# Seven products instead of eight for the keys and for half of the depth of queries and gates

## The chip, the core and the metric

The kernel runs on one core of one Trainium2 chip. The metric is the time of one execution on the device in microseconds (us), taken as the median of several runs. A core has a matrix engine (TensorE, PE in the profile; its weight loads are a row of their own, PEld), a vector engine (VectorE, DVE), a scalar engine (ScalarE, ACT), GpSimd (POOL, hardly used here) and SyncE (SP), whose queue issues all the DMA transfers of this kernel. Each engine takes its instructions strictly in the order in which they were put. Matmuls read SBUF and add into banks of PSUM (128 partitions x 512 fp32 values each); DVE and ACT read the banks.

## What is computed

A sequence of 512 tokens of width 2048 goes through an mLSTM layer, then a band-attention layer with 16 heads of 128. All is fp32. The part around the change:

```python
hkv = modulate(rmsnorm(x, kv_g), kmod[:, :D_MODEL], kmod[:, D_MODEL:])
kv = hkv @ kv_w
k_sh = kv[..., :B_WIDTH].reshape(Bn, S, B_HEADS, B_DH)
v_sh = kv[..., B_WIDTH:].reshape(Bn, S, B_HEADS, B_DH)
...
qz = h @ w_in
q = qz[..., :B_WIDTH].reshape(B, S, B_HEADS, B_DH)
z = qz[..., B_WIDTH:]
o = chunk_band_attention(q, k, v, rel_table)
y = o.reshape(B, S, B_WIDTH) * jax.nn.silu(z)
return y @ w_out
```

`kv_w` and `w_in` of this layer are 2048 x 4096 each, `w_out` is 2048 x 2048.

## The kernel before

**Products.** Every fp32 operand of a large product is split in two: `split` (L152) has ACT cast it to fp32r (the high part, `hi`) and DVE subtract that from it (the low part, `lo`). `mm3` (L176) then makes three matmuls, hi x hi, hi x lo and lo x hi. A matmul takes 128 x 128 weights and streams up to 512 columns past them.

**Weights.** All weights lie in DRAM in the order of use (`stream`, L42). `wpiece` (L158) loads the next piece, 128 x 1024 fp32 (512 KB), into one of three `raw` buffers, and splits it into one of three `hi` and `lo` buffers. It is put ahead of other work by a priority (`AHEAD`), so a scheduler, which fixes the order on each engine when the program is built, lets it run up to three pieces ahead of PE.

**Projections.** `proj_a` (L192) makes a transposed tile: 128 output columns x 512 tokens in one PSUM bank, over 16 blocks of depth with 128 each, two pieces of eight blocks. `proj_b` (L195) makes four (or two) tiles of 128 tokens x 512 output columns at once, two blocks of depth to a piece. `psP` has five banks for such tiles, `psA` three for all else.

**Stages** (the time of each in the profiled execution stands in the table below): start and the mLSTM heads; its output projection (`rows`); *values* of groups 0 and 1, in two pairs of token tiles (`values`, L680), among which the second half of the tokens is turned and made into `hkv` (`turned`, L621); *keys*, 16 tiles by `proj_a` (L694); values of groups 2 and 3; meanwhile `h2`, the input of queries and gates, is made tile by tile (L701), in the slots that `hkv` leaves free; *attention*, a loop over heads (L792); the output projection and the end. Keys and values of all heads stay in SBUF (`kv`).

In a turn `h` of the loop stand `queries(h)` (one tile by `proj_a`), `mixed(h - 2)` (weights times values, gate, the split of `y2`), `weights(h - 1)` (scores `ps_s`, softmax), `gated(h)` (another tile by `proj_a`, silu) and `flipped(h - 1)` (transposes `ps_t`, splits of the weights and the values).

## Time and profile before

| | us |
|---|---|
| median of 3 runs (2862.17 to 2864.84) | 2862.86 |
| the profiled execution | 2862.53 |
| its span, first to last instruction | 2860.7 |
| output projection of the mLSTM | 1543 to 1896 |
| values, groups 0 and 1 | 1896 to 1989 |
| keys | 1989 to 2163 |
| values, groups 2 and 3 | 2163 to 2250 |
| attention | 2250 to 2688 |
| output projection and end | 2688 to 2861 |

In rows of the profile, a name such as `ps_k<-hkv,wh` says what is written and what is read, without buffer numbers; `128x512 f32` is partitions x elements. The mean time of an instruction is from its start to its end; matmuls are pipelined, so one starts before the one ahead of it has ended. Idle time in front of an instruction is put down to what released it.

### The profile page before, as it was taken

Reading aid. Unit: us, or ns where it says so; the run is one execution under the profiler, and the core shown is the slowest. Engines: PE = TensorE matmul, PEld = TensorE weight load, DVE = VectorE, ACT = ScalarE, POOL = GpSimd, SP = SyncE. Lnnn points to the kernel's source line nnn. Section 1 sums busy time; section 2 is a strip of 40 time slices with the busy share of each in tenths; the row PEclk is TensorE's granted clock in tenths of the full one; section 3 lists DMA queues with packets and bytes.
Section 4 is the critical chain, followed back from the end, with each engine's and each line's share of the span. In section 5 each row is a group of like instructions: output and inputs, shape, how many; then the busy total and the mean of one; then the engine's idle time right before and its main releaser. Section 6 shows DMA issues by size and latency. Waiting matters only on the chain.

```text
span 2860.7 us, 33028 instructions
## 1 busy us (share of the span) xinstructions
PE 2832.2 (99%) x12770; PEld 2340.4 (82%) x12770; DVE 1587.4 (55%) x2358; ACT 1126.1 (39%) x1646; POOL 0.2 (0%) x4
## 2 busy tenths in 40 slices
PE   7999999999999999999999999999999999999998
PEld 5787888888888888888888888888888888888887
DVE  7986747466375564764735445575222455545425
ACT  4244524333242342332424345454222445545323
POOL 0000000000000000000000000000000000000000
PEclk9999999999999999999999999999999999999999
DMA  8874546456456464554635557786222322222334
GB/s 307 310 235 159 192 158 211 168 173 209 155 184 213 136 225 155 195 203 154 209 108 177 180 195 238 231 274 217 96 99 103 138 92 86 90 91 88 137 103 173
DMA packets 154950, 491.09 MB, mean 172 GB/s; under 512 B 17012, under 2 KB 26132, under 8 KB 154280
## 3 DMA queue, kind: packets, MB, share of 16 engines
q1 hardware_dynamic: 154792, 488.98, 50.2%
q8 instruction: 100, 1.64, 0.2%
q14 instruction: 58, 0.48, 0.0%
HBM read 467.89 MB, written 26.26 MB: 173 GB/s over the span
## 4 chain that ended last, share of the span: by engine, by line
PE 93%; DVE 3%; DMA 2%; issue 1%; ACT 1%; SPq 0%; DVEq 0%; ACTq 0%
PE ps_y L174 17%; PE ps_z L174 17%; PE ps_o L174 12%; PE ps_v L174 12%; PE ps_qk L174 9%; PE ps_q L174 6%; PE ps_k L174 6%; PE ps_kv L174 5%; PE ps_l L174 2%; PE ps_s L174 2%; PE ps_n L174 2%; PE ps_lead L174 1%; DVE wl L154 1%; DVE ada L245 1%; DMA wr<-in_wst 1%
## 5 line engine op out<-in xcount | busy, mean ns | idle before, releaser
L154 DVE TENSOR_TENSOR wl<-wr,wh 128x1024 fp32r<-128x1024 f32 (+3 forms) x586 | 680.4, 1162 | 1078.1 <-ACT wh L153 1077.6
L153 ACT CAST wh<-wr 128x1024 fp32r<-128x1024 f32 (+3 forms) x586 | 587.3, 1003 | 1433.0 <-PE ps_y L174 235.6
L174 PE MATMUL ps_y<-wh,y 128*128 128x512 f32 x1536 | 475.2, 390 | 0.0
L174 PE MATMUL ps_z<-h,wh 128*128 128x512 f32 x1408 | 433.9, 389 | 0.0
L174 PEld LDWEIGHTS ps_y<-wh,y 128*128 128x128 f32 x1536 | 288.2, 188 | 59.2
L174 PE MATMUL ps_v<-wh,h 128*128 128x512 f32 x1024 | 317.2, 389 | 0.0
L174 PEld LDWEIGHTS ps_z<-h,wh 128*128 128x128 f32 x1408 | 263.3, 188 | 54.0
L174 PE MATMUL ps_y<-wl,y 128*128 128x512 f32 x768 | 299.1, 389 | 0.0
L174 PE MATMUL ps_o<-h,wh 128*128 128x512 f32 x896 | 276.2, 389 | 0.0
L174 PE MATMUL ps_z<-h,wl 128*128 128x512 f32 x704 | 274.1, 389 | 0.0
L174 PE MATMUL ps_qk<-h,wh 128*128 128x512 f32 x768 | 237.8, 391 | 0.0
L174 PEld LDWEIGHTS ps_v<-wh,h 128*128 128x128 f32 x1024 | 192.1, 188 | 39.8
L174 PE MATMUL ps_v<-wl,h 128*128 128x512 f32 x512 | 199.4, 390 | 0.0
L174 PEld LDWEIGHTS ps_o<-h,wh 128*128 128x128 f32 x896 | 167.3, 188 | 34.1
L245 DVE CUSTOM_DVE_ANT_0 ada<-ada,scB,mod 128x1024 f32<-128x1024 f32 x128 | 164.1, 1282 | 24.2 <-DMA ada<-in_adaT 22.7
L174 PE MATMUL ps_o<-h,wl 128*128 128x512 f32 x448 | 174.4, 389 | 0.0
L174 PEld LDWEIGHTS ps_y<-wl,y 128*128 128x128 f32 x768 | 144.2, 188 | 30.0
L245 DVE CUSTOM_DVE_ANT_0 ada<-ada,scB,cl 128x1024 f32<-128x1024 f32 x128 | 164.0, 1282 | 6.0 <-DMA ada<-in_adaT 5.9
L174 PEld LDWEIGHTS ps_qk<-h,wh 128*128 128x128 f32 x768 | 143.2, 188 | 29.1
L174 PE MATMUL ps_q<-h,wh 128*128 128x512 f32 x512 | 159.3, 392 | 0.0
L174 PE MATMUL ps_kv<-wh,hkv 128*128 128x512 f32 x512 | 159.2, 391 | 0.0
L174 PE MATMUL ps_k<-hkv,wh 128*128 128x512 f32 x512 | 157.5, 389 | 0.0
(216 smaller groups left out, 3389.0 us busy)
## 6 DMA issues: line engine op xcount, KB each, us to landing
wr<-in_wst SPq DMA_DIRECT2D x520, 512.0 KB, 3.3
ada<-in_adaT SPq DMA_DIRECT2D x256, 512.0 KB, 5.4
yr<-ysc SPq DMA_DIRECT2D x16, 512.0 KB, 3.6
wr<-in_wst SPq DMA_DIRECT2D x30, 256.0 KB, 4.5
ysc<-so SPq DMA_DIRECT2D x28, 256.0 KB, 5.3
wr<-in_wst SPq DMA_DIRECT2D x16, 384.0 KB, 5.4
bsc<-in_ext SPq DMA_DIRECT2D x16, 320.0 KB, 6.1
xt<-in_xT SPq DMA_DIRECT2D x4, 1024.0 KB, 7.0
```

Of the source, the lines that this page charges most:

```text
L153: nc.scalar.copy(hi, src)
L154: nc.vector.tensor_tensor(lo, src, hi.bitcast(F32), op=ALU.subtract)
L174: nc.tensor.matmul(ps, a, b, start=start, stop=stop)
L245: pin(nc.vector.tensor_tensor_reduce(at, at, scB[:, j * D // 2 : (j + 1) * D // 2], 1.0, mod[:, i : i + 1] if j else col(CB + i), ALU.mult ...
```

## The change

Take two blocks of depth and two tiles of output columns as a 2 x 2 matrix of weight blocks, and the two blocks of depth and two halves of the tokens as a 2 x 2 matrix of inputs. Their product takes eight block products; in Winograd's form of Strassen's method it takes seven, of sums and differences of the blocks. A block product is a matmul of 128 x 128 weights and 256 tokens, here three of them (`mm3`).

`KEY_PAIRS` says for each of the eight pairs of key tiles how many of the eight pairs of depth blocks are done with seven products: 4, 6, and then all 8. `ATT_PAIRS` says the same for the pair of query and gate tile of a head: 4 of 8. The rest goes as before, with matmuls of 512 columns, into two of the same banks.

- `proj_s` makes a pair of tiles in four banks D, C, A and B, and puts the result together in an SBUF tile `z` (one copy and five sums).
- `half_sums`, called by `key_sums` and `query_sums`, makes the four sums of input halves for a pair of depth blocks and splits them. Four pairs for the keys are made among the values, the other four among the first two pairs of keys; four for the attention among values 2 and 3.
- `wpiece(mat, ns, ...)` makes the three weight sums of `ns` pairs in a piece with three subtractions and additions on DVE, and splits them.
- Room in SBUF: keys, values and `y2` go to DRAM and are loaded again per head (`fetch`) or per two heads (`y2_tile`); `ones_r`, `maskd`, `x2` and the pools `wp`, `rp`, `t2` move.
- The loop over heads: `queries(h, mid)` makes query and gate as one pair; `mixed(h - 2)` and `weights(h - 1)` are called in it ahead of its third piece, `flipped(h - 1)` behind it. `gated` is gone.

The diff, cut to its core:

```diff
+KEY_PAIRS = [4, 6, 8, 8, 8, 8, 8, 8]
+ATT_PAIRS = 4
...
+def pair_pieces(f):
+    sk, nk = list(range(f)), list(range(f, KT // 2))
+    n = min(len(sk), len(nk))
+    out = [([a], [b]) for a, b in zip(sk, nk)]
+    out[1:1] = [([], nk[i : i + 2]) for i in range(n, len(nk), 2)]
+    return out + [(sk[i : i + 2], []) for i in range(n, len(sk), 2)]
...
+            if ns:
+                w = ns * P
+                t = pl.tile([P, 3 * w], F32, tag="ws", name=f"ws{i}", bufs=2)
+                nc.vector.tensor_tensor(t[:, : 2 * w], raw[:, w : 3 * w], raw[:, : 2 * w], op=ALU.subtract)
+                nc.vector.tensor_tensor(raw[:, w : 2 * w], t[:, w : 2 * w], raw[:, :w], op=ALU.add)
+                nc.vector.tensor_tensor(t[:, 2 * w :], raw[:, 3 * w : 4 * w], raw[:, w : 2 * w], op=ALU.subtract)
             hi = wp.tile([P, 1024], F32R, tag="hi", name=f"wh{i}")[:, :n]
             lo = wp.tile([P, 1024], F32R, tag="lo", name=f"wl{i}")[:, :n]
             split(hi, lo, raw)
+            if ns:
+                sh = pl.tile([P, 3 * w], F32R, tag="wsh", name=f"wsh{i}", bufs=bufs)
+                sl = pl.tile([P, 3 * w], F32R, tag="wsl", name=f"wsl{i}", bufs=bufs)
+                split(sh, sl, t)
+                return hi, lo, sh, sl
...
+    def proj_s(mat, xs, ss, f, z, name, pl, bufs, at={}):
+        D, C, A, B = [newp(f"ps_{n}{name}") for n in "dcab"]
...
+            def seven():
+                end = i == len(pieces) - 1
+                for ps, cols, b0, x, xcols, last in (
+                    (D, h1_, ns, lambda k: ss[k][1], h0, False),
+                    (D, h0, 0, lambda k: xs[2 * k], h0, end),
+                    (C, h0, -2 * ns, lambda k: ss[k][0], h1_, False),
+                    (C, h1_, -3 * ns, lambda k: ss[k][0], h0, end),
+                    (A, h0, 3 * ns, lambda k: xs[2 * k + 1], h0, False),
+                    (A, h1_, -ns, lambda k: xs[2 * k + 1], h1_, end),
+                    (B, h0, 2 * ns, lambda k: ss[k][1], h1_, end),
+                ):
...
+                    for j, k in enumerate(sk):
+                        acc(ps, cols, b0 + j, x(k), xcols, last and j == ns - 1)
...
+        with tc.high_priority(AHEAD):
+            nc.scalar.copy(z[:, 0, :], D[:, h0])
+            nc.vector.tensor_tensor(z[:, 3, :], z[:, 0, :], D[:, h1_], op=ALU.add)
+            nc.vector.tensor_tensor(
+                z[:, 1:3, :], z[:, 3:4, :].to_broadcast([P, 2, 256]), C.rearrange("p (a t) -> p a t", a=2), op=ALU.add
+            )
+            nc.vector.tensor_tensor(z[:, 3, :], z[:, 1, :], C[:, h1_], op=ALU.add)
+            nc.vector.tensor_tensor(z[:, 0:2, :], z[:, 0:2, :], A.rearrange("p (a t) -> p a t", a=2), op=ALU.add)
...
+    def half_sums(raw, tmp, pl, tag, name, bufs=KT):
+        (a11, a21), (a12, a22) = ((r[:, :256], r[:, 256:]) for r in raw)
+        (s1, s3), (s2, s4) = ((t[:, :256], t[:, 256:]) for t in tmp)
+        nc.vector.tensor_tensor(s1, a21, a22, op=ALU.add)
+        nc.vector.tensor_tensor(s3, a11, a21, op=ALU.subtract)
+        nc.vector.tensor_tensor(s2, a22, s3, op=ALU.subtract)
+        nc.vector.tensor_tensor(s4, a12, s2, op=ALU.subtract)
...
+            s = pl.tile([P, 2, S], F32R, tag=tag, name=f"{name}_{i}", bufs=bufs)
+            split(s[:, 0, :], s[:, 1, :], t)
...
-        for p, m in zip(pv, ms):
-            for j in range(4):
-                nc.scalar.copy(kv[4 * g + j][:, 1, m * P : (m + 1) * P], p[:, j * P : (j + 1) * P])
...
+            nc.scalar.copy(v, p)
+            nc.sync.dma_start(vsc[g][:, :, m * P : (m + 1) * P], v.rearrange("p (j t) -> p j t", j=4))
...
-    for i in range(KT):
-        ps = newp(f"ps_k{i}")
-        proj_a("kv_w", hkv, ps)
-        nc.scalar.copy(kv[i][:, 0, :], ps)
...
+    for i in range(KT // 2):
+        z = zp.tile([P, 4, 256], F32, tag="z", name=f"zk{i}")
+        ready = len(hs)
+        at = {j: lambda: key_sums(len(hs)) for j in (1, 2)} if ready < KT // 2 else {}
+        assert ready == KEY_PAIRS[i]
+        proj_s("kv_w", hkv, hs, ready, z, f"k{i}", zp, 2, at)
+        nc.sync.dma_start(ksc[i].rearrange("p a t -> p (a t)"), z.rearrange("p a t -> p (a t)"))
...
-    def queries(h):
-        ps = newp(f"ps_q{h}")
-        proj_a("b_w_in", h2, ps)
...
+    def queries(h, mid):
+        if h < BH - 1:
+            fetch(h + 1)
+        z = at.tile([P, 4, 256], F32, tag="z", name=f"z{h}", bufs=2)
+        proj_s("b_w_in", h2, h2s, ATT_PAIRS, z, f"z{h}", at, 3, {2: mid})
...
-        t = kp.tile([P, 2, S], F32R, tag="k", name=f"y2_{h}")
-        split(t[:, 0, :], t[:, 1, :], sz)
-        y2.append(t)
+        nc.sync.dma_start(y2c[h // 2][:, h % 2, :], sz)
...
+    def y2_tile(k):
+        while len(y2) <= k:
+            i = len(y2) // 2
+            raw = wp.tile([P, 2, S], F32, tag="raw", name=f"y2r{i}")
+            nc.sync.dma_start(raw, y2c[i])
+            for j in range(2):
+                t = xp.tile([P, 2, S], F32R, tag="x", name=f"y2_{i}_{j}")
+                split(t[:, 0, :], t[:, 1, :], raw[:, j, :])
+                y2.append(t)
+        return y2[k]
```

More of the change, by code (lines that the diff above doesn't have):

```diff
@@ L39, with add, tile_s @@
 LATER += [DK, DK + P, V0 // 2 + DK, V0 // 2 + DK + P]
+KEY_PAIRS = [4, 6, 8, 8, 8, 8, 8, 8]
[6 more added lines that the diff above has]
+    return out + [(sk[i : i + 2], []) for i in range(n, len(sk), 2)]
 def stream():
     out = []
+    def add(mat, kts, cs):
+        out.append((mat, [(k, c, n) for k in kts for c, n in cs]))
     def tile_a(mat, col, kts=KT):
         for k in range(0, kts, 8):
-            out.append((mat, list(range(k, k + 8)), [(col, P)]))
+            add(mat, range(k, k + 8), [(col, P)])
     def tile_b(mat, col, kts=KT):
         for k in range(0, kts, 2):
-            out.append((mat, [k, k + 1], [(col, 512)]))
+            add(mat, [k, k + 1], [(col, 512)])
+    def tile_s(mat, c1, c2, f):
+        for sk, nk in pair_pieces(f):
+            blocks = [(2 * k + i, c, P) for i, c in ((0, c1), (0, c2), (1, c2), (1, c1)) for k in sk]
+            out.append((mat, blocks + [(2 * k + i, c, P) for k in nk for i in range(2) for c in (c1, c2)]))
     for k0, k1 in BLOCKS:
         for k in range(k0, k1):
-            out.append(("a_w_in", [k], [(c, P) for c in LEAD]))
+            add("a_w_in", [k], [(c, P) for c in LEAD])
         for c in LATER:
-            out.append(("a_w_in", list(range(k0, k1)), [(c, P)]))
+            add("a_w_in", range(k0, k1), [(c, P)])
     for h in range(NH):
@@ L74, in stream @@
             tile_b("kv_w", D + g * 512)
-    for i in range(KT):
-        tile_a("kv_w", i * P)
+    for i in range(KT // 2):
+        tile_s("kv_w", 2 * i * P, (2 * i + 1) * P, KEY_PAIRS[i])
     for g in range(2, 4):
@@ L79, in stream @@
     for h in range(BH):
-        tile_a("b_w_in", h * P)
-        tile_a("b_w_in", D + h * P)
+        tile_s("b_w_in", h * P, D + h * P, ATT_PAIRS)
     for g in range(3):
@@ L86, in stream @@
     return out
-def sizes():
-    return [len(kts) * sum(n for _, n in cs) for _, kts, cs in stream()]
 CB = 0
@@ L111, in hybrid_trunk @@
     dram = ctx.enter_context(tc.tile_pool(name="scr", bufs=1, space=bass.MemoryType.DRAM))
-    wp = ctx.enter_context(tc.tile_pool(name="wp", bufs=3))
     xp = ctx.enter_context(tc.tile_pool(name="xp", bufs=KT))
@@ L115, in hybrid_trunk, with pool @@
     psA = ctx.enter_context(tc.tile_pool(name="psA", bufs=3, space=bass.MemoryType.PSUM))
-    def pool(name, bufs=1):
-        return tc.tile_pool(name=name, bufs=bufs, reuse_waits="tile")
+    def pool(name, bufs=1, **kw):
+        return tc.tile_pool(name=name, bufs=bufs, reuse_waits="tile", **kw)
+    wp = ctx.enter_context(tc.tile_pool(name="wp", bufs=3, side="right"))
     ysc = dram.tile([NH, P, 4, S], F32, name="ysc")
@@ L125, in hybrid_trunk @@
     bsc = dram.tile([BH, P, EXTW], F32, name="bsc")
+    ksc = [dram.tile([P, 2, S], F32, name=f"ksc{i}") for i in range(BH // 2)]
+    vsc = [dram.tile([P, 4, S], F32, name=f"vsc{g}") for g in range(4)]
+    y2c = [dram.tile([P, 2, S], F32, name=f"y2c{i}") for i in range(BH // 2)]
     cl = const.tile([P, NCOL], F32, name="cl")
-    kcs = const.tile([P, 272], F32, name="kcs")
+    kcs = const.tile([P, 144], F32, name="kcs")
     ones_f = const.tile([P, P], F32, name="ones_f")
-    ones_r = const.tile([P, P], F32R, name="ones_r")
     cst = const.tile([P, 4], F32, name="cst")
@@ L138, in hybrid_trunk @@
     nc.vector.memset(ones_f, 1.0)
-    nc.vector.memset(ones_r.bitcast(F32), 1.0)
     nc.vector.memset(cst[:, 0:1], EPS)
@@ L143, in hybrid_trunk @@
     ident = kcs[:, 0:128]
-    maskd = kcs[:, 128:256]
-    sel = kcs[:32, 256:272]
+    sel = kcs[:32, 128:144]
     def col(i):
@@ L156, in hybrid_trunk, with wpiece @@
     ahead = [0]
-    def wpiece(mat):
+    def wpiece(mat, ns=0, pl=None, bufs=2):
         i, at = wpos
-        m, kts, cs = order[i]
+        m, blocks = order[i]
         assert m == mat
-        n = len(kts) * sum(w for _, w in cs)
+        n = sum(w for _, _, w in blocks)
         wpos[:] = i + 1, at + P * n
@@ L167, in wpiece @@
             nc.sync.dma_start(raw, wst[at : at + P * n].rearrange("(p n) -> p n", p=P))
+            out = []
+            if ns:
[4 more added lines that the diff above has]
+                nc.vector.tensor_tensor(t[:, 2 * w :], raw[:, 3 * w : 4 * w], raw[:, w : 2 * w], op=ALU.subtract)
             hi = wp.tile([P, 1024], F32R, tag="hi", name=f"wh{i}")[:, :n]
@@ L214, in proj_b, with acc, eight @@
             held.clear()
+    def proj_s(mat, xs, ss, f, z, name, pl, bufs, at={}):
+        D, C, A, B = [newp(f"ps_{n}{name}") for n in "dcab"]
+        pieces = pair_pieces(f)
+        begun = set()
+        h0, h1_ = slice(0, 256), slice(256, 512)
+        for i, (sk, nk) in enumerate(pieces):
+            if i in at:
+                at[i]()
+            ns = len(sk)
+            parts = wpiece(mat, ns, pl, bufs)
+            def acc(ps, cols, b, x, xcols, last):
+                start = id(ps) not in begun
+                begun.add(id(ps))
+                hi, lo = parts[:2] if b >= 0 else parts[2:]
+                w0 = (b if b >= 0 else b + 3 * ns) * P
+                w = slice(w0, w0 + P)
+                mm3(ps[:, cols], hi[:, w], lo[:, w], x[:, 0, xcols], x[:, 1, xcols], start, last)
+            def eight():
+                for m, k in enumerate(nk):
+                    for j in range(2):
+                        for t, ps in enumerate((A, B)):
+                            acc(ps, slice(0, S), 4 * ns + 4 * m + 2 * j + t, xs[2 * k + j], slice(0, S), False)
+            def seven():
[9 more added lines that the diff above has]
+                ):
+                    if i == 0 and ps is B:
+                        eight()
+                    for j, k in enumerate(sk):
+                        acc(ps, cols, b0 + j, x(k), xcols, last and j == ns - 1)
+            if i:
+                eight()
+            seven()
+        with tc.high_priority(AHEAD):
[6 more added lines that the diff above has]
+            nc.vector.tensor_tensor(z[:, 0:2, :], z[:, 0:2, :], A.rearrange("p (a t) -> p a t", a=2), op=ALU.add)
+            if f < KT // 2:
+                nc.vector.tensor_tensor(z[:, 2:4, :], z[:, 2:4, :], B.rearrange("p (a t) -> p a t", a=2), op=ALU.add)
+            else:
+                nc.vector.tensor_tensor(z[:, 2, :], z[:, 2, :], B[:, h0], op=ALU.add)
@@ new lines, in half_sums @@
+    def half_sums(raw, tmp, pl, tag, name, bufs=KT):
[5 more added lines that the diff above has]
+        nc.vector.tensor_tensor(s4, a12, s2, op=ALU.subtract)
+        out = []
+        for i, t in enumerate(tmp):
+            s = pl.tile([P, 2, S], F32R, tag=tag, name=f"{name}_{i}", bufs=bufs)
+            split(s[:, 0, :], s[:, 1, :], t)
+            out.append(s)
+        return out
@@ L270, in hybrid_trunk @@
             pin(nc.sync.dma_start(cl, cols))
-    pin(nc.sync.dma_start(kcs, kc))
+    pin(nc.sync.dma_start(kcs, kc[:, :144]))
     early = [ada_load(KT, j, ap_, ADA_BUFS, pin) for j in range(2)]
@@ L337, in hybrid_trunk @@
     aT = hp.tile([P, 4, NH], F32, name="aT")
+    ones_r = hp.tile([P, P], F32R, name="ones_r")
+    nc.vector.memset(ones_r.bitcast(F32), 1.0)
+    maskd = hp.tile([P, P], F32, name="maskd")
+    nc.sync.dma_start(maskd, kc[:, 144:272])
     graw = tp.tile([P, KT, 16], F32, tag="t", name="graw")
@@ L560, in hybrid_trunk @@
     kp = kst.enter_context(pool("kp", bufs=KT))
+    tst = ExitStack()
+    tp = tst.enter_context(pool("t2", bufs=6, side="right"))
     rst = ExitStack()
-    rp = rst.enter_context(pool("rp", bufs=12))
-    tst = ExitStack()
-    tp = tst.enter_context(pool("t2", bufs=6))
+    rp = rst.enter_context(pool("rp", bufs=12, side="right"))
     ys = []
@@ L675, in hybrid_trunk @@
             rows(g, ms, ys, at)
-    kv = [kp.tile([P, 2, S], F32, tag="k", name=f"kv{h}") for h in range(BH)]
     def values(g, ms, at={}):
@@ L682, in values, with key_sums @@
         proj_b("kv_w", hkv, pv, ms=ms, at=at)
-        for p, m in zip(pv, ms):
-            for j in range(4):
-                nc.scalar.copy(kv[4 * g + j][:, 1, m * P : (m + 1) * P], p[:, j * P : (j + 1) * P])
+        for i, (p, m) in enumerate(zip(pv, ms)):
+            if g < 2:
+                v = tp.tile([P, S], F32, tag="t", name=f"v{g}_{m}")
+            else:
+                if i % 2 == 0:
+                    z = zp.tile([P, 2, S], F32, tag="z", name=f"v{g}_{m}")
+                v = z[:, i % 2, :]
+            nc.scalar.copy(v, p)
+            nc.sync.dma_start(vsc[g][:, :, m * P : (m + 1) * P], v.rearrange("p (j t) -> p j t", j=4))
+    hs = []
+    def key_sums(k):
+        raw = [kept(2 * k + i, slice(0, S)) for i in range(2)]
+        for i, r in enumerate(raw):
+            c = KT + 2 * k + i
+            nc.scalar.activation(r, r, AF.Identity, bias=mod[:, 80 + c : 81 + c], scale=amul[:, c : c + 1])
+        tmp = [tp.tile([P, S], F32, tag="t", name=f"hs{k}_{i}") for i in range(2)]
+        hs.append(half_sums(raw, tmp, kp, "k", f"hs{k}"))
     with tc.high_priority(AHEAD):
@@ L692, in hybrid_trunk, with query_sums @@
             turn = {4 * i: lambda i=i: turned(1, [i], True) for i in range(4)} if pair == 0 and g == 1 else {}
+            if pair:
+                turn = {k: lambda k=k: key_sums(2 * g + k // 8) for k in (4, 12)}
             values(g, ms, turn)
-    for i in range(KT):
-        ps = newp(f"ps_k{i}")
-        proj_a("kv_w", hkv, ps)
-        nc.scalar.copy(kv[i][:, 0, :], ps)
+    rst.close()
+    zst = ExitStack()
+    zp = zst.enter_context(pool("zp", bufs=2, side="right"))
+    for i in range(KT // 2):
+        z = zp.tile([P, 4, 256], F32, tag="z", name=f"zk{i}")
[4 more added lines that the diff above has]
+        nc.sync.dma_start(ksc[i].rearrange("p a t -> p (a t)"), z.rearrange("p a t -> p (a t)"))
+    kst.close()
+    ast = ExitStack()
+    kq = ast.enter_context(pool("kq"))
+    h2s = []
+    def query_sums(k):
+        raw = [kept(2 * k + i, slice(0, S)) for i in range(2)]
+        for i, r in enumerate(raw):
+            c = 2 * k + i
+            nc.scalar.activation(r, r, AF.Identity, bias=mod[:, 48 + c : 49 + c], scale=amul[:, 2 * KT + c : 2 * KT + c + 1])
+        tmp = [tp.tile([P, S], F32, tag="t", name=f"h2s{k}_{i}") for i in range(2)]
+        h2s.append(half_sums(raw, tmp, kq, "h2s", f"h2s{k}", 2 * ATT_PAIRS))
     for g in range(2, 4):
-        values(g, range(4))
+        n = -(-ATT_PAIRS // 2)
+        ks = [k for k in range((g - 2) * n, min((g - 1) * n, ATT_PAIRS))]
+        values(g, range(4), {2 + 4 * i: lambda k=k: query_sums(k) for i, k in enumerate(ks)})
     h2 = []
@@ L708, in hybrid_trunk, with fetch @@
         h2.append(t)
+    zst.close()
     tst.close()
-    rst.close()
-    ast = ExitStack()
     at = ast.enter_context(pool("att"))
-    y2 = []
-    def queries(h):
-        ps = newp(f"ps_q{h}")
-        proj_a("b_w_in", h2, ps)
-        q0 = at.tile([P, P], F32, tag="q0", name=f"q0_{h}")
-        nc.scalar.copy(q0, ps[:, :P])
+    kv = []
+    def fetch(h):
+        t = kq.tile([P, 2, S], F32, tag="kv", name=f"kv{h}", bufs=3)
+        nc.sync.dma_start(t[:, 0, :], ksc[h // 2][:, h % 2, :])
+        nc.sync.dma_start(t[:, 1, :], vsc[h // 4][:, h % 4, :])
+        kv.append(t)
+    fetch(0)
+    def queries(h, mid):
[3 more added lines that the diff above has]
+        proj_s("b_w_in", h2, h2s, ATT_PAIRS, z, f"z{h}", at, 3, {2: mid})
+        qz = z.rearrange("p a t -> p (a t)")
         q = at.tile([P, 2, 384], F32R, tag="q", name=f"q{h}", bufs=2)
-        split(q[:, 0, :], q[:, 1, :], ps[:, P:])
+        split(q[:, 0, :], q[:, 1, :], qz[:, P:S])
+        sz = qz[:, S:]
+        nc.scalar.activation(sz, sz, AF.Silu)
         k = at.tile([P, 2, S], F32R, tag="kk", name=f"k{h}")
@@ L729, in queries @@
         nc.vector.memset(bias[:64, 448:512], NEG)
-        return q0, q, k, bias
+        return (qz[:, :P], q, k, bias), sz
     def weights(h, q0, q, k, bias):
@@ L771, in flipped @@
         return pts, v
-    def gated(h):
-        ps = newp(f"ps_z{h}")
-        proj_a("b_w_in", h2, ps)
-        sz = at.tile([P, S], F32, tag="sz", name=f"szb{h}", bufs=2)
-        nc.scalar.activation(sz, ps, AF.Silu)
-        return sz
     def mixed(h, pts, v, sz):
@@ L786, in mixed, with mid @@
         nc.vector.tensor_tensor(sz, ps, sz, op=ALU.mult)
-        t = kp.tile([P, 2, S], F32R, tag="k", name=f"y2_{h}")
-        split(t[:, 0, :], t[:, 1, :], sz)
-        y2.append(t)
+        nc.sync.dma_start(y2c[h // 2][:, h % 2, :], sz)
     qs, ptv, szs = {}, {}, {}
     for h in range(BH + 2):
-        if h < BH:
-            qs[h] = queries(h)
-        if h > 1:
-            mixed(h - 2, *ptv.pop(h - 2), szs.pop(h - 2))
-        if 0 < h <= BH:
-            pr = weights(h - 1, *qs.pop(h - 1))
-        if h < BH:
-            szs[h] = gated(h)
+        pr = []
+        def mid():
+            if h > 1:
+                mixed(h - 2, *ptv.pop(h - 2), szs.pop(h - 2))
+            if 0 < h <= BH:
+                pr.extend(weights(h - 1, *qs.pop(h - 1)))
+        if h < BH:
+            qs[h], szs[h] = queries(h, mid)
+        else:
+            mid()
         if 0 < h <= BH:
@@ L807, in hybrid_trunk @@
     op = ost.enter_context(pool("op", bufs=KT))
+    rp = ost.enter_context(pool("x2", bufs=8))
     yo = [[] for _ in range(4)]
@@ L810, in hybrid_trunk @@
     for m in range(4):
-        t = [xp.tile([P, 2, S], F32, tag="x", name=f"x2_{m}_{i}") for i in range(2)]
+        t = [rp.tile([P, 2, S], F32, tag="x2", name=f"x2_{m}_{i}") for i in range(2)]
         for i in range(2):
@@ L814, in hybrid_trunk @@
         x2.append([t[g // 2][:, g % 2, :] for g in range(4)])
+    y2 = []
+    def y2_tile(k):
[3 more added lines that the diff above has]
+            nc.sync.dma_start(raw, y2c[i])
+            for j in range(2):
+                t = xp.tile([P, 2, S], F32R, tag="x", name=f"y2_{i}_{j}")
+                split(t[:, 0, :], t[:, 1, :], raw[:, j, :])
+                y2.append(t)
+        return y2[k]
     def finish(m):
@@ L827, in hybrid_trunk @@
             at = {4: lambda: finish(0), 6: lambda: finish(1)} if pair == PAIRS[1] else {}
-            proj_b("b_w_out", y2, ps, ms=pair, at=at, late=3 if pair == PAIRS[1] else 0)
+            proj_b("b_w_out", y2_tile, ps, ms=pair, at=at, late=3 if pair == PAIRS[1] else 0)
             with tc.high_priority(AHEAD):
@@ L836, in hybrid_trunk @@
     ost.close()
-    kst.close()
 def layouts(x, c, ada_w, ada_b, g_pre, g_post, a_w_in, a_conv_w, a_conv_b, a_gate_b, a_g_head,
@@ L859, in layouts @@
         [
-            np.concatenate([mats[mat][k * P : (k + 1) * P, c0 : c0 + n] for k in kts for c0, n in cs], 1).ravel()
-            for mat, kts, cs in order
+            np.concatenate([mats[mat][k * P : (k + 1) * P, c0 : c0 + n] for k, c0, n in blocks], 1).ravel()
+            for mat, blocks in order
         ]
@@ L870, in layouts @@
     i = np.arange(P)
-    kc[:, 128:256] = np.where(i[None, :] >= i[:, None], 0.0, NEG)
-    kc[:32, 256:272] = np.tile(np.eye(16), (2, 1))
+    kc[:32, 128:144] = np.tile(np.eye(16), (2, 1))
+    kc[:, 144:272] = np.where(i[None, :] >= i[:, None], 0.0, NEG)
     return {
```

## The prediction

> **What bounds the kernel now.** I read the page first, then what the matmul engine (PE) waited for, then busy time by stage, then the stages' own instructions. The page's parts 1 and 4:

> ```profile
> PE 2832.2 (99%) x12770; PEld 2340.4 (82%) x12770; DVE 1587.4 (55%) x2358; ACT 1126.1 (39%) x1646; POOL 0.2 (0%) x4
> PE 93%; DVE 3%; DMA 2%; issue 1%; ACT 1%; SPq 0%; DVEq 0%; ACTq 0%
> ```

> PE is busy 99% of the span and is 93% of the chain that ended last. The view of waits, for PE, says where it stood still; all but those of ps_kv and ps_x L637 (0.4 us, not shown) lie in the first 250 us:

> ```profile
> PE ps_lead L174 <- ACT h L224: 7.8, 4, 3.4
> PE ps_x L174 <- DVE xsq L292: 4.1, 1, 4.1
> PE ps_kv L174 <- DVE wl L154: 0.8, 1, 0.8
> ```

> Busy time by stage (PE, PEld, DVE, ACT, POOL, clock, DMA share, GB/s): values g 0 and 1, keys, values g 2 and 3, attention.

> ```profile
> 1896.00:1989.00 93.00, 92.03 (x420) 75.52 (x419) 65.75 (x97) 54.77 (x108) 0.00 (x0) 1.00 0.76 254
> 1989.00:2163.00 174.00, 174.00 (x770) 144.06 (x769) 39.20 (x32) 41.60 (x51) 0.00 (x0) 1.00 0.29 100
> 2163.00:2250.00 87.00, 87.00 (x385) 72.05 (x384) 32.86 (x40) 30.70 (x60) 0.00 (x0) 1.00 0.37 127
> 2250.00:2688.00 438.00, 438.00 (x2100) 365.44 (x2099) 232.42 (x531) 220.24 (x392) 0.00 (x0) 1.00 0.29 99
> ```

> In keys and attention PE has no gap while VectorE (DVE) and ScalarE (ACT) are about a quarter to a half busy. So a change there is worth what it does to PE's stream of matmuls, as long as the new work of the others stays behind it.

> **The matmuls.** A matmul's printed duration is its latency; what counts is the distance from start to start. From the chain, 48 matmuls of 512 columns in one tile, and from the timeline of PE, stretches of six with 256 columns, each with the row after it:

> ```profile
> 2261.28 10.88 PE ps_z L174 x48
> ...
> 516.40 0.88 PE L174 MATMUL ps_s<-qk,qk 128*128 128x256 f32 x6
> 517.11 0.63 PE L174 MATMUL ps_o<-h,wh 128*128 128x512 f32 x2
> ...
> 2522.91 0.60 PE L174 MATMUL ps_s<-k,q 128*128 128x256 f32 x3
> 2523.35 0.63 PE L174 MATMUL ps_z<-h,wh 128*128 128x512 f32 x2
> ```

> 10.88/48 = 0.2267 us at 512 columns. 517.11 - 516.40 = 0.71 us for six, 0.119 us at 256 columns (three such stretches: 0.71 to 0.72). Half the columns cost a little more than half, 0.113. A pair of depth blocks for a pair of output tiles was 2 x 2 x 3 = 12 matmuls of 512 columns: 2.720 us. Now it is 7 x 3 = 21 of 256: 21 x 0.119 = 2.499 us. Each saves 0.221 us. Pairs on the new scheme: keys 4 + 6 + 6 x 8 = 58, attention 16 heads x 4 = 64, together 122; the instruction order of the changed program has 122 x 12 fewer and 122 x 21 more. Saving: 122 x 0.221 = **27.0 us**. Bounds: at exactly half of 0.2267 it would be 122 x (2.720 - 2.380) = 41.5 us; at the pace of the three after 2522.91, 0.44/3 = 0.147 us, it would be a loss of 122 x 0.367 = 44.8 us. I take the six: long stretches of one kind, as the new ones are; the three stand behind a matmul in plain fp32.

> [...]

> **VectorE and ScalarE.** Instructions back to back overlap by 0.08 us:

> ```profile
> 2496.50 0.68 DVE L786 TENSOR_TENSOR szb<-ps_o,szb 128x512 f32<-128x512 f32 x1
> 2497.10 0.28 DVE L745 SCALAR_TENSOR_TENSOR s<-ps_s,bias 128x128 f32<-128x128 f32 x1
> ```

> So with the mean rows of L154 and L745, less 0.08, an elementwise step on DVE costs 0.20 (128 columns), 0.33 (256), 0.46 (384), 0.60 (512), 0.88 (768), 1.14 (1024). Attention, per head: each of four weight pieces gains three sums (256, 128, 128) and one low part (384): 1.19; four make 4.8. Putting together the result is 2 x 0.33 + 3 x 0.60 = 2.5. The split of y2 (0.60) moves to the last stage. 232.42/16 = 14.5 becomes 21.2 us, against a period of PE of 2523.76 - 2497.10 (two L745 rows) = 26.7, less 4 x 0.221: 25.8. Keys, per full pair of tiles: 4 x (0.60 + 0.33 + 0.33 + 1.14 + 0.88) + 3 x 0.33 + 2 x 0.60 = 15.3 against 8 x 2.499 = 20.0. The first two pairs also make two half-sums each (4 x 0.33 + 2 x 0.60 = 2.5): 16.8 for the first, against 20.9. So neither stage is bound by DVE; ACT gains four casts of 384 columns (0.51 - 0.08) per head and loses y2's: 13.8 becomes about 15. This work I cost at nothing; the cover is PE's stream, and if it were gone it would cost 16 x 6.7 = 107 us in attention alone.

> Where it could show is the order of the queues. PSUM tiles pass from DVE to PE at three places in a head. Head's end: the last piece leaves D, C, A done 1.78, 1.07, 0.36 us before its end (15, 9, 3 matmuls); nine transposes (1.0) and six matmuls (0.71) follow before C of the next head needs D's bank, 3.5 us after D was done; the copy and one sum take 0.7, behind at most one 1.14 step: fits. Scores: s_2 reuses the bank of ps_o, 1.5 us after ps_o ended; before its product (0.68) DVE finishes a low part whose cast began when PE left the piece before ps_o: ready with some 0.1 us to spare. The fourth transpose waits for the low part of the first with as little. I take 0.1 us a head, **1.6 us**; bounds 0 and 0.5 x 16 = 8.

> **Start of attention.** Before, PE passes from values to queries without a gap:

> ```profile
> 2250.01 0.39 PE L174 MATMUL ps_kv<-wh,hkv 128*128 128x512 f32 x1
> 2250.24 0.62 PE L174 MATMUL ps_q<-h,wh 128*128 128x512 f32 x2
> ```

> since weight splits run ahead. In the changed order, head 0's first weight sums stand on DVE behind the low part of h2's last tile, which takes hkv's last slot, and so behind the last ps_kv matmul; PE has nothing else. From that matmul's end at 2250.40: copy of the value tile 0.58, cast of h2 0.62, its low part 0.69 (to 2252.2), two sums of 256 and one of 128 (2253.1), cast of 1024 columns 1.05 (2254.1), its low part 1.22 behind the key split (2255.4). Five matmuls (0.6) need only the cast. Idle: 2255.4 - 2250.24 - 0.6 = **4.6 us**; bounds 3.5 (without the key split and one sum) and 6.

> **DMA and SyncE's queue.** Values and keys go to DRAM and back, y2 too: 12.6 MB out, as much in. In keys and attention the share is 0.29, so they hide. In values g 0 and 1 it is 0.76, PE waited 0.8 us once, and eight value stores of 512-byte runs (nearest row: nsc, 256 KB, 4.4 us to land) and eight loads for half-sums join, some queued ahead of weights: **1 us**, bounds 0 and 4. At the end of attention two y2 splits stand on DVE between the sums of the last head, and wait for a load (yr, 512 KB: 3.6 us) that waits for a weight buffer; PE needs the banks they hold up: **1 us**, bounds 0 and 3. y2's loads then come one a piece (two depth blocks, 24 x 0.2267 = 5.4 us), under cover of it. Moving ones_r, maskd and pools leaves the order on PE up to ps_kv as it was: 0.

> **Sum.** Profiled run 2862.5 (span 2860.7 and 1.8 around it) - 27.0 + 4.6 + 1.6 + 1 + 1 = 2843.7. The median of the runs, 2862.9, is 0.3 above that run: **2844**.

> **Rivals.**
> *Queues decide (slower).* A split waits for its cast: DVE idled 18.6 us before the 16 first pt splits, 1.16 each. If six of a head's eight weight splits wait so, DVE needs 21.2 + 7.0 = 28.2 against 25.8: 2.4 x 16 = 39 us; 2862.9 - 27.0 + 4.6 + 39 = 2879. It decides from (28.2 - 2.4 - 21.2) = 4.6 us of waits a head, and eats the gain at 1.4 us of stall a head. For it: DVE at 82%, thin margins. Against: the changed order puts other steps between most casts and their low parts. 10%.
> *Half-width matmuls run at the three's pace*, 0.147 (slower): 2862.9 + 44.8 + 8.2 = 2916. For it: stretches of 45 and more are nowhere in the trace. Against: every stretch of six. 4%. At 0.1295 a pair costs as before.
> *No load is hidden behind a half-width matmul* (slower): the load's row is 0.188 us; 122 x (21 x 0.188 - 2.720) = 150, 3021 with the 8.2. 2%, for the six have six loads of 0.188 in 0.71 us. [...]
> *Stage changes cost more* (their upper bounds, 6 + 8 + 4 + 3 for 8.2): 2862.9 - 27.0 + 21 = 2857, nearly no change. 11%.
> *Half costs exactly half*: 2862.9 - 41.5 + 8.2 = 2830. 5%, as the overhead of 0.006 us shows in all stretches.
> *It doesn't do what it says*: ruled out by the counts above.

> **Numbers.** Forecast 68%, its own range 2836 to 2854. What differs by less than 0.2% (5.7 us) can't be told from no change. Faster: 68 + 5 + half of 11 = 78%; same 6%; slower 10 + 4 + 2 = 16%. The range leaves out the two slow rivals on PE's pace, most of the queue rival and part of the fastest: 2832 to 2866.

> **What will show it.** 24 half-width matmuls in 2.86 us in ps_dk and ps_ck; a key pair in 20.0 us; head period 25.8; one PE gap of 4 to 5 us at the first ps_dz, released by ACT; PE waits under 0.5 us elsewhere. Wrong, if PE waits for DVE or ACT in every head, or if the pace in long stretches is over 0.125.

## The result, and the profile after

| | us |
|---|---|
| median after, 18 runs (2854.03 to 2861.89) | 2857.58 |
| median before, 18 runs (2862.09 to 2866.54) | 2864.03 |
| ratio | 0.9979, 95% interval 0.9972 to 0.9986 |
| the profiled execution after, and its span | 2856.81, 2854.9 |

Faster by 6.4 us, a difference of 0.2% that is clear of the noise (the interval ends below 1), as forecast in sign; 19 us had been forecast. The page's parts 1 and 4 after:

```profile
PE 2813.5 (99%) x13868; PEld 2374.5 (83%) x13868; DVE 1826.3 (64%) x2934; ACT 1195.7 (42%) x1734; POOL 0.2 (0%) x4
PE 92%; DVE 4%; DMA 1%; issue 1%; ACT 1%; DVEq 0%; SPq 0%; ACTq 0%
```

The shares look as before. What differs stands in the view of PE's waits (us in total, times, longest). Of these rows only that of ps_lead was there before, with 7.8 us; the other four are new:

```profile
PE ps_lead L205 <- ACT h L329: 8.6, 4, 3.4
PE ps_dz L205 <- ACT wh L171: 5.5, 1, 5.5
...
PE ps_t L918 <- DVE pt L172: 2.5, 3, 1.4
PE ps_ck L205 <- DVE zk L295: 2.4, 1, 2.4
...
PE ps_s L205 <- DVE z L936: 0.6, 1, 0.6
```

One gap at the start of attention (ps_dz), one behind the first pair of keys (ps_ck), and stalls in single heads (ps_t, ps_s). Busy time by stage after: values 0 and 1, keys, values 2 and 3, the gap, attention.

```profile
1897.00:1990.80 93.80, 92.06 (x417) 74.58 (x416) 71.89 (x117) 61.73 (x102) 0.00 (x0) 1.00 0.82 266
1990.80:2158.30 167.50, 164.71 (x1291) 160.86 (x1290) 137.13 (x229) 74.21 (x96) 0.00 (x0) 0.99 0.46 154
2158.30:2245.50 87.20, 87.20 (x386) 71.93 (x384) 42.08 (x62) 33.25 (x46) 0.00 (x0) 1.00 0.55 181
2245.50:2251.00 5.50, 0.04 (x1) 0.00 (x0) 3.56 (x9) 3.12 (x7) 0.00 (x0) 0.73 0.66 197
2251.00:2664.20 413.20, 409.97 (x2580) 368.32 (x2581) 333.61 (x817) 228.38 (x417) 0.00 (x0) 1.00 0.39 122
```

The table goes by first matmuls of the stages, and the last column is a kernel that comes last below:

| us | before | after | all three edits |
|---|---|---|---|
| up to the values | 1896.62 | 1896.96 | 1896.96 |
| values 0 and 1 | 92.51 | 93.86 | 93.93 |
| keys | 174.08 | 167.49 | 163.81 |
| values 2 and 3, and the gap behind them | 87.04 | 92.72 | 87.07 |
| attention, up to its last stage | 419.42 | 413.18 | 407.35 |
| output projection and end | 191.04 | 190.67 | 190.65 |

Keys and attention gain 6.6 and 6.2 us, half of what the matmuls alone should give, and the gap takes 5.7 back.

The half-width matmuls (256 columns) keep the pace that the prediction took, or nearly. From the chain that ended last, in the keys:

```profile
2042.56 1.44 PE ps_dk L205 x12
2043.99 1.44 PE ps_ck L205 x12
```

1.44/12 = 0.120 us, at 0.119 forecast. What had not been seen at all is the pace behind the gaps. Stretches of 3.41 us in and behind both gaps, laid so that the granted clock (the third column from the end) changes at their ends:

```profile
2012.48:2015.90 3.42, 1.01 (x8) 0.81 (x8) 3.42 (x8) 1.56 (x4) 0.00 (x0) 1.00 0.42 131
2015.90:2019.31 3.41, 3.03 (x13) 2.66 (x12) 3.41 (x7) 2.52 (x4) 0.00 (x0) 0.50 0.50 177
2019.31:2022.72 3.41, 3.41 (x18) 2.83 (x18) 3.41 (x7) 2.02 (x4) 0.00 (x0) 1.00 0.83 308
2244.59:2248.00 3.41, 0.95 (x5) 0.45 (x3) 1.98 (x5) 1.94 (x4) 0.00 (x0) 1.00 0.75 207
2248.00:2251.42 3.42, 0.39 (x2) 0.39 (x2) 1.99 (x7) 2.42 (x5) 0.00 (x0) 0.50 0.57 179
2251.42:2254.83 3.41, 3.41 (x17) 3.29 (x17) 3.41 (x7) 1.33 (x2) 0.00 (x0) 0.50 0.42 133
2254.83:2258.24 3.41, 3.41 (x19) 2.93 (x19) 3.41 (x10) 1.46 (x2) 0.00 (x0) 1.00 0.53 174
```

At a clock of 0.50 half-width matmuls start 0.213 us apart (seven steps in the 1.49 from 2253.10 to 2254.59) instead of 0.120. In the keys that lasted 3.41 us, of which PE worked 3.03: a loss of at most 1.5 us. At the start of attention PE worked the last 3.80 us of such a stretch, from the first ps_dz at 2251.03 to 2254.83: a loss of 1.9 us.

PE did not stand idle for a whole stretch ahead of either fall of the clock: of the 3.42 and 3.41 us before 2015.90 and 2248.00 it worked 1.01 and 0.95, and in the keys the gap lasted 2.4 us. The clock was back at 1.00 behind a stretch at 0.50 with 3.03 us of work in the keys, and behind one with 3.41 at the start of attention.

### The profile page after: what moved, and what is told of

It reads as the page before. It is cut to its first block, busy times and chain, and to the rows that moved or that the text cites. A ratio compares the mean times of both kernels' runs of the same rounds, so it can differ in the third digit from the quotient of the medians.

```text
span 2854.9 us, 36484 instructions
## 1 busy us (share of the span) xinstructions
PE 2813.5 (99%) x13868; PEld 2374.5 (83%) x13868; DVE 1826.3 (64%) x2934; ACT 1195.7 (42%) x1734; POOL 0.2 (0%) x4
## 4 chain that ended last, share of the span: by engine, by line
PE 92%; DVE 4%; DMA 1%; issue 1%; ACT 1%; DVEq 0%; SPq 0%; ACTq 0%
PE ps_y L205 18%; PE ps_v L205 12%; PE ps_o L205 12%; PE ps_z L205 11%; PE ps_qk L205 9%; PE ps_kv L205 5%; PE ps_az L205 4%; PE ps_bz L205 4%; PE ps_l L205 2%; PE ps_n L205 2%; PE ps_s L205 2%; PE ps_ak L205 2%; PE ps_dk L205 1%; PE ps_dz L205 1%; PE ps_ck L205 1%; PE ps_cz L205 1%
## 5 line engine op out<-in xcount | busy, mean ns | idle before, releaser
L205 PE MATMUL ps_z<-h,wh 128*128 128x512 f32 x896 | 275.9, 389 | 0.0
L205 PEld LDWEIGHTS ps_z<-h,wh 128*128 128x128 f32 x896 | 168.2, 188 | 34.8
L205 PE MATMUL ps_z<-h,wl 128*128 128x512 f32 x448 | 174.3, 389 | 0.0
L205 PE MATMUL ps_qk<-h,wl 128*128 128x512 f32 x384 | 149.5, 389 | 0.0
L171 ACT CAST wsh<-ws 128x384 fp32r<-128x384 f32 (+1 forms) x96 | 57.1, 595 | 146.4 <-PE ps_az L205 69.3
```

What stands on the lines that cost most here:

```text
L171: nc.scalar.copy(hi, src)
L205: nc.tensor.matmul(ps, a, b, start=start, stop=stop)
```

## Experiments

Each kernel is the changed one with the edit shown, unless said otherwise. Ratios are to the kernel before, run beside it on the same chip. Three chips were used; the kernel before took 2864.25 us on that of the first four rows, 2864.67 on that of the next four and 2865.19 on that of the last three.

| | us | ratio, 95% interval |
|---|---|---|
| half sums 4 to 7 left out | 2855.84 | 0.9970, 0.9959 to 0.9981 |
| head 0's tiles low | 2857.08 | 0.9974, 0.9965 to 0.9984 |
| gap filled | 2853.86 | 0.9965, 0.9952 to 0.9977 |
| eight products everywhere | 2864.90 | 1.0002, 0.9993 to 1.0011 |
| attention only | 2860.34 | 0.9987, 0.9978 to 0.9996 |
| keys only | 2858.48 | 0.9976, 0.9967 to 0.9986 |
| all half sums among values | 2861.64 | 0.9988, 0.9979 to 0.9997 |
| weight sums low | 2849.78 | 0.9945, 0.9931 to 0.9958 |
| + key sums later | 2846.05 | 0.9933, 0.9920 to 0.9945 |
| + memset on GpSimd | 2847.19 | 0.9935, 0.9923 to 0.9948 |
| all three | 2843.61 | 0.9922, 0.9909 to 0.9936 |

### Eight products everywhere

```diff
-KEY_PAIRS = [4, 6, 8, 8, 8, 8, 8, 8]
-ATT_PAIRS = 4
+KEY_PAIRS = [0] * 8
+ATT_PAIRS = 0
```

with banks A and B alone, copied to `z`, and no half sums.

> All pairs of depth blocks are done with eight products of 512 columns, no half sums and no weight sums; the rest of the change stays (pairs of tiles in one go, keys, values and y2 through DRAM, moved pools, the loop over heads). Theory A: what is missing from the forecast lies in stalls and half clock caused by the sums, so the rest costs next to nothing: 2863 to 2866, with no PE gap over 1 us after 1900 us. Rival B: the rest of the change (transfers to DRAM and back, moved pools, pairs) costs several us: 2868 or more, and these are in every stage.

2864.9 us, the time of the kernel before. Keys take 174.08 us and attention 419.58, as before (174.08 and 419.42). So the rest of the change (pairs, transfers through DRAM, moved pools) costs at most some 3 us by the interval, and theory A stands: what is missing lies with the sums.

### Attention only, keys only

```diff
-KEY_PAIRS = [4, 6, 8, 8, 8, 8, 8, 8]
+KEY_PAIRS = [0] * 8
```

> Seven products in the attention alone (4 of 8 pairs of depth blocks in each head); the keys with eight products and without half sums. Theory A (half-width matmuls at 0.120 us save 0.20 us a pair; the rest of the forecast is lost in three stalls and the half clock behind them): 64 x 0.20 = 12.8 us gained against the kernel with eight everywhere (2864.9), 7.4 lost at the start of attention and 3.1 in stalls inside heads: 2862 to 2863. Rival B (each pair saves less, or the heads are bound by VectorE throughout): 2866 or more. Rival C (the two parts disturb each other only when together): 2855 or less.

> Seven products in the keys alone; queries and gates with eight, without their weight sums and half sums. Theory A: 58 x 0.20 = 11.6 us gained against 2864.9, 4.6 lost behind the first pair of keys and about 1 among the values: 2859. No PE gap at the start of attention. Rival B (the pairs' saving is smaller than 0.20 us): 2862 or more.

(`ATT_PAIRS = 0` in the second; in both, the part without sums goes as in the run before.) The keys alone came as expected: 2858.5, with 1.5 us of gap before ps_ck and none at the start of attention. The attention alone was 2 us better than expected, 2860.3: its gap was 3.9 us, not 5.5 (why is open). Against 2864.9 the two gain 4.6 and 6.4 us; together the changed kernel gains 7.3. Rivals B fall, and rival C with its 2855. The 3.7 us between 11.0 and 7.3 are hardly more than what such medians can tell; but the profiles show most of them at places: the keys take 166.86 us without the other part and 167.49 with it, values 2 and 3 with the gap 91.07 and 92.72, attention 412.64 and 413.18. So each part seems to make the other stall a little more, as far as single profiles can tell.

### The gap behind the first keys

ScalarE in the changed kernel (start, duration, idle time before and its releaser):

```profile
2002.50 1.52 ACT L806 ACTIVATE xt<-xt,mod,amul 128x512 f32<-128x512 f32 x2 [4.92 <-DMA xt<-nsc]
...
2012.14 1.52 ACT L806 ACTIVATE xt<-xt,mod,amul 128x512 f32<-128x512 f32 x2
2013.57 0.35 ACT L294 COPY zk<-ps_dk 128x256 f32<-128x256 f32 x1
```

It stands 4.9 us for the loads of half sums, catches up, and copies D only at 2013.57, though PE's last matmul into D began at 2010.26. VectorE's sum on the copy follows at 2015.00, behind a low part and a first step of half sums and a weight sum, and PE starts ps_ck at 2015.47.

```diff
     def key_sums(k):
+        if k >= 4:
+            hs.append(hs[k - 4])
+            return
```

> The half sums of the depth pairs 4 to 7 of the keys (two loads, two activations, four sums, two splits each) are left out, and those of pairs 0 to 3 are used twice. PE's matmuls stay as they are. Theory A: in the changed kernel PE stands still for 2.4 us before the first ps_ck of the second pair of keys, because the copy and first sum of the first pair's D stand on ScalarE and VectorE behind these half sums, and the 21 matmuls behind that gap run at half clock (2.2 us more). Then both go: keys 167.5 -> about 163 us, the whole 2857.6 -> 2853. Rival B: the banks pass from VectorE to PE too slowly whatever stands ahead of it (copy, sum, five banks for four tiles); then the gap stays within 0.5 us and so does the time.

The gap shrank from 2.4 to 1.3 us and did not go: the order of the program had changed, and ScalarE now stood for the loads of the queries' half sums, which had moved up into the place:

```profile
2011.12 1.52 ACT L841 ACTIVATE xt<-xt,mod,amul 128x512 f32<-128x512 f32 x2 [3.74 <-DMA xt<-nsc]
2012.55 0.35 ACT L294 COPY zk<-ps_dk 128x256 f32<-128x256 f32 x1
```

So it doesn't decide between A and B. Behind this gap of 1.3 us the clock stayed at 1.00.

```diff
-KEY_PAIRS = [4, 6, 8, 8, 8, 8, 8, 8]
+KEY_PAIRS = [8] * 8
...
-                turn = {k: lambda k=k: key_sums(2 * g + k // 8) for k in (4, 12)}
+                turn = {k: lambda k=k: key_sums(4 * g + k // 4) for k in (2, 6, 10, 14)}
```

> All eight pairs of half sums of the keys are made among the values (two to each eight pieces instead of one), so all eight pairs of keys use seven products on all eight depth pairs, and no half sum stands in the first two pairs of keys. Theory A: PE's gap behind the first pair of keys (2.4 us, with 2.2 us of half clock behind it) comes from ScalarE standing 4.9 us for the loads of the half sums, with the activations on them ahead of the copy of D. Then no gap there; 6 more pairs at 0.20 us; the values lose at most 2 us more to the loads: 2857.6 - 4.6 - 1.2 + 1 = 2853. Rival B (the banks of the first pair pass too slowly for another reason): a gap before the second pair's ps_ck stays.

A miss: 2861.6. The keys took 171.69 us, 4.2 more than in the changed kernel. PE no longer waits for a bank behind the first pair, but in the first pair for the half sums themselves, and once for a bank that ScalarE had not yet copied a value tile out of:

```profile
PE ps_ck L205 <- ACT hs L171: 2.2, 2, 1.2
PE ps_bk L205 <- ACT v L797: 1.4, 1, 1.4
...
PE ps_dk L205 <- DVE hs L172: 1.0, 1, 1.0
```

The last six activations of the half sums come one after another from 2002.75 to 2013.89, as the loads land, and the copy of the value tile waits behind them until 2013.79. Among the values the DMA share is 0.84 here, after 0.82 in the changed kernel. Both theories had left that out. The other way, later, and on top of the kernel with the weight sums low (next section):

```diff
-KEY_PAIRS = [4, 6, 8, 8, 8, 8, 8, 8]
+KEY_PAIRS = [4, 4, 6, 8, 8, 8, 8, 8]
...
-        at = {j: lambda: key_sums(len(hs)) for j in (1, 2)} if ready < KT // 2 else {}
+        at = {j: lambda: key_sums(len(hs)) for j in (1, 2)} if i and ready < KT // 2 else {}
```

(and the copy and sum of D and these activations are kept in program order).

> On top of the kernel with the weight sums' tiles in the pool below (2849.8): the half sums of the keys' depth pairs 4 to 7 are called one pair of tiles later (4, 4, 6, then 8 depth pairs with seven products), so that in ScalarE's order two activations instead of six stand ahead of the copy of the first D. Theory A (ScalarE, standing for the loads of the half sums ahead of that copy, makes the gap): the 2.0 us of gap and the 2.2 of half clock behind it go, four pairs of 0.20 us are given up: 2849.8 - 4.2 + 0.8 = 2846.4. Rival B (the banks themselves): gap as before, 2850.6.

2846.05, as A said. The keys take 163.85 us instead of 166.88, with no gap. (The rest of the 3.7 us lies in attention, 410.12 us for 411.80, which the edit does not touch: so much can differ between two executions.) ScalarE stands for no load there:

```profile
2009.57 1.52 ACT L807 ACTIVATE xt<-xt,mod,amul 128x512 f32<-128x512 f32 x2
...
2012.57 0.36 ACT L295 COPY zk<-ps_dk 128x256 f32<-128x256 f32 x1
```

Rival B falls: the same banks pass in time. The edit removes the wait for the loads and four activations at once; how much each of these and the fixed order weighs stays open.

### The start of attention

ScalarE in the changed kernel, behind the last value tile (PE's last ps_kv began at 2245.15, its first ps_dz at 2251.03):

```profile
2249.00 0.62 ACT L171 CAST k<-kv 128x512 fp32r<-128x512 f32 x1 [2.32 <-DMA vsc<-v]
2249.52 0.51 ACT L171 CAST vv<-kv 128x384 fp32r<-128x384 f32 x1
2249.94 1.04 ACT L171 CAST wh<-wr 128x1024 fp32r<-128x1024 f32 x1
```

The weight sums that the cast of `wh` needs were done at 2248.9. It comes a microsecond later, behind the cast of head 0's keys: that tile lies in room which a store of the last values still reads.

```diff
     at = ast.enter_context(pool("att"))
+    k0 = at.tile([P, 2, S], F32R, tag="kk", name="k0")
+    v0 = at.tile([P, 2, 384], F32R, tag="vv", name="vv0")
```

> Head 0's tiles for the split keys and values are laid at the bottom of the attention pool, where no store out of the last value tiles is still reading. Theory A: in the changed kernel ScalarE stands for 2.3 us at the cast of head 0's keys, which waits for that store, and the cast of the first weights stands behind it. Then the cast of weights starts when the weight sums are done, about 1.5 us earlier, and the PE gap ahead of the first ps_dz goes from 5.5 to about 4.0 us: 2857.6 -> 2856. Rival B, the prediction's own chain (weight sums on VectorE behind the last low part of h2 set the gap): the gap stays at 5.5 us.

The gap fell to 3.9 us, as A said, so the store is part of it. The time hardly moved (2857.08): the clock came back at about 2254.8 (estimated from the mean of 0.96 in the second row), as it had at 2254.83, so PE started 2 us earlier and spent them at half clock.

```profile
2249.00:2254.50 5.50, 5.50 (x22) 5.09 (x23) 5.50 (x12) 3.14 (x5) 0.00 (x0) 0.50 0.61 182
2254.50:2258.00 3.50, 3.50 (x18) 2.94 (x17) 2.54 (x7) 0.87 (x1) 0.00 (x0) 0.96 0.63 211
```

Is it the clock?

```diff
+    idle = newa("ps_idle")
+    for i in range(24):
+        mm(idle, h2[0][:, 0, :P], h2[0][:, 0, :], i == 0, i == 23)
     qs, ptv, szs = {}, {}, {}
```

> 24 matmuls of 512 columns without use (h2 with itself, into a bank that nobody reads) are put on PE between the last ps_kv and the first ps_dz, 5.4 us of work in a gap of 5.5 us. Theory A: the first 20 half-width matmuls behind the gap take 0.213 instead of 0.120 us because PE's clock is lowered after standing still (granted clock 0.52 in that stretch); PE kept busy, they run at 0.120 and the time falls by about 1.9 us, 2857.6 -> 2856. Rival B: they are slow because each waits for a low part or a weight sum; then they stay at 0.2 us and the time stays, or rises by what the filler sticks out.

With PE kept busy, the same first piece of attention runs at full clock:

```profile
2254.40:2257.70 3.30, 3.28 (x22) 3.04 (x23) 3.30 (x5) 1.74 (x3) 0.00 (x0) 1.00 0.31 89
```

ps_dz and ps_az start 0.12 us apart there, so theory A holds: they waited for no low part. The median, 3.7 us less, is from five runs, of which the profiled one was the slowest (2857.20); the stage from ps_dz on is 2.8 us shorter in the profile, of which 1.9 are the clock.

Then the gap itself:

```diff
-        proj_s("b_w_in", h2, h2s, ATT_PAIRS, z, f"z{h}", at, 3, {2: mid})
+        proj_s("b_w_in", h2, h2s, ATT_PAIRS, z, f"z{h}", kq, 3, {2: mid})
```

> The tiles of the weight sums of the attention come from the pool below (room that is free since the end of the keys), so that head 0's weights can be prepared before the values end; nothing else is changed. Theory A: the gap of 5.5 us ahead of the first ps_dz and the 1.9 us of half clock behind it go: 2857.6 -> 2850 to 2851. Rival B: the gap is needed for something else (banks, h2's last tiles) and stays over 3 us: 2855 or more.

2849.78: the weight sums now stand among the values, and the first ps_dz follows the last ps_kv in 0.23 us. Values 2 and 3 with the gap take 87.07 instead of 92.72 us. Rival B falls. VectorE makes the first sums at 2229.18, and the low part of h2's last tile only at 2248.24, when PE is already in attention: what had tied the sums to the end of the values was the room of their tiles.

### Stalls inside heads

The rows of the bias's memset, VectorE's idle time before it (us, times), after:

```profile
L886 DVE MEMSET bias<- x16: 112/112/112, 2254.6 to 2633.4; 64x64 f32 x16
its engine sat idle before it (us, times) until:
  DMA bias<-bsc: 7.8, 9
```

Before the change the last row was

```profile
  DMA bias<-bsc: 0.2, 1
```

The load now lands 3.8 us after its issue (median) where it took 2.6, and VectorE stands for it in front of a memset of 0.11 us, with all that is queued behind it. Three of PE's four stalls of over 0.1 us in the heads (ends at 2380.5, 2564.0 and 2642.0) come some 9 us behind such waits of 1.7, 2.3 and 1.2 us (ends at 2371.4, 2554.9 and 2633.4); the fourth ends 11 us after the first.

```diff
-        nc.vector.memset(bias[:64, 448:512], NEG)
+        nc.gpsimd.memset(bias[:64, 448:512], NEG)
```

on top of the weight sums low:

> On top of the kernel with the weight sums' tiles in the pool below (2849.8): the memset of a corner of each head's bias goes from VectorE to GpSimd, which has nothing else to do. Theory A: the stalls inside four heads (2.1 us before ps_t, 1.1 before ps_s) begin with VectorE standing at this memset for the load of the bias (7.8 us in 9 of 16 heads in the changed kernel), and six or seven microseconds of work behind it then come late; without it the stalls fall below 1 us together: 2847. Rival B: VectorE, busy 81% of the attention, is late there whatever it waits for: stalls within 0.5 us of before, 2849.5 to 2850.

2847.19. The waits of ps_t fell from 2.1 us to below the rows shown, that of ps_s stayed at 0.9, in one head; attention fell from 411.80 to 408.48 us. All eight profiles with seven products in attention and the memset on VectorE show waits of ps_t, 0.9 to 3.3 us; the two with the memset on GpSimd show none. A holds, but for that one head.

### All three

> All three edits together: tiles of the weight sums in the pool below, half sums of keys one pair later, memset of the bias on GpSimd. If the three losses are separate, as theory A has it, they add: 2857.6 - 7.8 - 3.4 - 2.8 = 2843.6, which is the forecast with its terms of 4.6 and 1.6 us gone and a pair's saving at 0.20. If they share a cause (VectorE's load as a whole), one stall takes the place of another: 2847 or more.

2843.61 us. From 2849.78 the two later edits gain 3.7 and 2.6 alone and 6.2 together. Medians of five runs don't carry this by themselves (their intervals overlap), but the stages do: the keys take 163.85 us with the one edit and 163.81 with both, attention 408.48 with the other and 407.35 with both. So the losses are separate. In the keys and in attention PE is busy without a break (1990.90 to 2154.80 and 2241.80 to 2649.30):

```profile
1990.90:2154.80 163.90, 163.90 (x1256) 158.76 (x1255) 132.07 (x225) 72.99 (x97) 0.00 (x0) 1.00 0.47 158
...
2241.80:2649.30 407.50, 407.50 (x2582) 366.86 (x2581) 331.05 (x793) 228.23 (x419) 3.36 (x16) 1.00 0.40 124
```

This version beats both kernels.

## Why the prediction was right and wrong

Each term of its sum, against the stages' times (the kernel with all three edits gives the matmuls without stalls):

| term, us | forecast | measured |
|---|---|---|
| the matmuls | -27.0 | -23.1 |
| keys, sums on VectorE and ScalarE | 0 | +4.4 |
| start of attention | +4.6 | +7.6 |
| handover inside heads | +1.6 | +3.9 |
| values 0 and 1 | +1 | +1.4 |
| end of attention | +1 | -0.4 |
| first 1897 us | 0 | +0.3 |
| sum | -18.8 | -5.9 |

The two profiled spans differ by 5.8. That the right column adds up to this is no check of it: its terms are differences of the same stages' times. Of the 12.9 us between the two sums the keys make 4.4, the matmuls 3.9, the start of attention 3.0 and the heads 2.3.

*The matmuls.* Without stalls 54 pairs of keys saved 174.08 - 163.81 = 10.3 us and 64 of attention 419.42 - 407.35 = 12.1: 0.19 each, not 0.221; 122 x 0.189 = 23.1. Of the 0.03, two thirds are the pace: 21 x 0.120 = 2.520 for 2.499. Six matmuls in 0.71 to 0.72 us could not tell 0.119 from 0.120. So 24 took 2.88 us (2.86 forecast) and a full pair of keys 4 x 5.04 = 20.2 (20.0). In the keys, the pairs that stay with eight products also take 2.75 instead of 2.72 us. The two banks between which they now go back and forth are not the reason: with eight products everywhere they do so too, and take 2.72. The first five matmuls of 512 columns behind half-width ones are slower, 0.229 to 0.236 us; why is open.

*Keys.* The step that failed first is "This work I cost at nothing; the cover is PE's stream". It compared sums of busy time: 16.8 us on VectorE against 20.9 on PE. VectorE does fit in, 137 us of 167.5. But ScalarE took its queue in order, and the first pair's held six activations on loads for which it stood 4.92 us: the copy of D, behind them, came at 2013.57, 3.31 us after PE's last matmul into D had begun. The three places at which the prediction looked for banks that pass too late lie all inside a head of attention, none in the keys. Keys lost 167.49 - (174.08 - 58 x 0.189) = 4.4 us: 2.4 of gap, at most 1.5 of half clock, the rest short waits behind.

*Start of attention.* "Idle: 2255.4 - 2250.24 - 0.6 = 4.6" had the right place, and in the changed kernel its chain held up to the weight sums: 3.3 us from the end of the last ps_kv to theirs, with the sums of two pieces in a row, 2253.1 - 2250.40 = 2.7 forecast with those of one (and one of these put at 256 columns, where it has 128: 0.13 us too much). That the sums stand there at all was no order that the work needs, as the run with the weight sums low shows. As a price it failed in two ways: the cast of the keys, queued ahead and waiting for a store, was not in the chain (1.6 us by the run with head 0's tiles low), and the half clock behind the gap was not in it either (1.9). 92.72 - 87.07 + 1.9 = 7.6 lies above the upper bound of 6.

*Inside heads.* 0.1 us in each was wrong in kind: 413.18 - 407.35 - 1.9 = 3.9 us, nearly all in four turns of the loop. Period and other steps were right: from ps_o to ps_o 25.9 us where nothing stalls, 25.8 forecast. A wait was there that the profile of before could show only as 0.2 us: VectorE at the bias's memset.

*The rest* came as forecast: values 0 and 1 lost 1.4 for 1, the end cost nothing, the moved pools nothing.

*The rivals.* "Stage changes cost more", 2857 at 11%, is the number that came, but by luck: the keys, 4.4 of the loss, and the smaller saving of the matmuls are not in it. "Queues decide" is the kind of cause that was at work, but not in every head, and at waits for loads, not for casts. Matmuls at 0.147, loads not hidden, and exactly half are ruled out by the 0.120. Neither of the two signs of being wrong that the prediction named came up: the losses sit in single places.

The forecast of 2844 and the 2843.61 of the last kernel agree in part by chance: the terms of 4.6 and 1.6 are gone there, and the matmuls save less on 118 pairs.

## What to carry to other kernels

Whether work is hidden is not told by sums of busy time per stage. Look on each engine for each instruction that waits for a transfer, and for what stands behind it: a memset, a cast, an activation on a load, a tile in room that a store still reads. And a gap on PE can cost more than itself: in the changed kernel, behind steps of 3.41 us in which PE stood idle for 2.41 and 2.46 (next section), the clock was at 0.50 for 3.41 and 6.83 us, which cost up to 1.5 us behind one of the gaps and 1.9 behind the other. Close the gap, or give PE something to do in it; a gap made shorter may gain nothing, as 3.9 us instead of 5.5 at the start of attention gained 0.5 us in the median.
